# MLP of a two-layer decoder: the fourth block's down-projection feature by feature, the other three turned by VectorE and DMA

## The chip, the cores and the metric

The kernel runs on one core of a Trainium2 chip. The time is device microseconds (us) of that core, median of the runs shown. All numbers of the trace come from one profiled execution of the kernel.

## What is computed

A decoder of two layers over 256 tokens of 2048 features, all in float32. Each layer is a mixer (attention of one kind in layer 0, of another in layer 1), an MLP with squared ReLU, and a gated addition of a per-layer embedding. The part that the change touches is this, for each layer i:

```python
hn = rmsnorm(h, mlp_norm_g[i])
h = h + jnp.square(jax.nn.relu(hn @ mlp_w1[i])) @ mlp_w2[i]
gate = jax.nn.sigmoid(rmsnorm(h, ple_norm_g[i]) @ ple_w_gate[i])
h = h + (p[i] @ ple_w_proj[i]) * gate
```

mlp_w1 is 2048 x 8192, mlp_w2 is 8192 x 2048, ple_w_gate is 2048 x 2048 and ple_w_proj 256 x 2048.

## The kernel before

**Layout.** The residual stream x lies feature by feature: 16 tiles of 128 features by 256 tokens, two of them side by side in each of eight tiles xp[0] to xp[7] (L179, L180). Activations that enter a matmul are split in a high part in the type float32r and a low part (the rest), side by side in one tile of 512 columns (`split_to` L469, `renorm` L331). A product is high x high + high x low + low x high, all added up in PSUM.

**Weights.** Every weight is read once, in chunks of 128 x 1024 floats (512 KB). `load` (L198) fetches a chunk into one of four raw buffers through SP's queue; `copy` (L210) casts it on ScalarE to the high part (six buffers), and `sub` (L218) takes the low part on VectorE (five buffers). `Program.run` (L111) writes out the order by hand: for each chunk it first issues loads (at most seven chunks ahead, and only into a raw buffer whose subtraction has been issued), casts (four ahead) and subtractions (three ahead), then `advance` (L81) lets every follow-up generator that is under way take one step, then it issues the chunk's matmuls, and the follow-ups of a finished tile begin at the next chunk's step. A `yield` in a follow-up is thus a delay of one chunk. Nothing is reordered afterwards: each engine takes its instructions in that order, and SP takes its DMAs in that order too, each waiting for what it needs before the next one is looked at.

**Two forms of a projection.** `quad` (L376) goes feature by feature: the weights are the stationary operand, and four tiles of 128 features fill four PSUM banks over its chunks. A chunk gives 8 pairs of matmuls, one of 512 columns (L352: high weights by both parts of the activation) and one of 256 (L354: low weights by the high part). A bank ends with its two halves still to be added. `token_major` (L421) goes token by token: the activation is stationary and the weights move; two banks hold two halves of 128 tokens by 512 features, and a chunk gives 12 matmuls of 512 columns (L442). PSUM has two sets of four banks ("mm" and "at"), and each quad or token-major quarter takes the set that the one before didn't (`four_banks` L365, `two_banks` L415).

**The MLP** (`mlp`, L493) goes through the 8192 hidden features in four blocks of 2048. In each block four quads of eight chunks (w1) make 16 tiles h, and then four token-major quarters of eight chunks (w2) take these into 512 output features each. The sum over the blocks lies token by token in a tile y of 2 x 2048 floats a partition: ScalarE writes it for the first block (L504), VectorE adds the later ones (L502). In the fourth block `down` goes on for each quarter: eight transposes on TensorE against the identity (L513) into two banks of the other set, two adds to x of 512 columns on VectorE (L517), and then for each tile of x the renewed split and square for the next norm (`renorm`: L316 and L242 on ScalarE, L322 and L250 on VectorE). The transposes of a quarter are issued behind the second chunk of the next one, and those of the last quarter behind the second chunk of the next stage.

**The stage behind it** (`ple`, L559) goes through four quarters of: a quad of one chunk (the embedding's projection, pj tiles in pool "h", L723) and a quad of eight chunks (the gate). The gate's quad reads the renewed splits of x, and its norm's factor is worked out from chunk 4 on.

**The output projections of the mixers** (`out_proj`, L482) are quads whose follow-up is `add_to_x` (L474: two adds of 256 columns from PSUM into x) and `renorm`, with the third and fourth tile one step later (`late=True`). The profile has them in 449.81 to 483.09 us (layer 0, four chunks a quad).

Of the kernel before, what the change touches and what calls it, by code (L numbers as in the profile page):

```python
# [10 lines left out]
F32 = mybir.dt.float32  # L11
# [4 lines left out]
P = 128  # L16
D = 2048
T = 256
# [10 lines left out]
NFB = 4  # L29
# [9 lines left out]
G_ATTN, G_MLP, G_PLE, G_KV, G_FIN = 0, 2, 4, 6, 7  # L39
# [105 lines left out]
def kernel(ctx: ExitStack, tc: tile.TileContext, a: dict, out: bass.AP):  # L145
    nc = tc.nc
    ctx.enter_context(tc.manual_schedule())
    prog = Program()
# [4 lines left out]
    tmp = ctx.enter_context(tc.tile_pool(name="tmp", bufs=2))  # L153
    xap = ctx.enter_context(tc.tile_pool(name="xa", bufs=KT))
    wpool = ctx.enter_context(tc.tile_pool(name="w", bufs=4))
    pspool = ctx.enter_context(tc.tile_pool(name="ps", bufs=1, space=bass.MemoryType.PSUM))

    cur = {}

    def open_pool(key):  # L160
        es = ExitStack()
        cur[key] = es.enter_context(tc.tile_pool(name=key, reuse_waits="tile", bufs=1))
        cur[key + "/es"] = es

    def close_pool(key):
        cur.pop(key)
        cur.pop(key + "/es").close()

    def bank():
        return pspool.tile([P, 512], F32, tag="mm", name="mm", bufs=4)  # L170

    def banks2():
        return pspool.tile([P, 2, 512], F32, tag="at", name="at", bufs=2)
# [5 lines left out]
    xp = [xg0[:, :2 * T]] + [xpool.tile([P, 2 * T], F32, name=f"x{j}") for j in range(1, KT // 2)]  # L179
# [151 lines left out]
    def renorm(k, gi, to, norm):  # L331

        t = split_hi(k, gi)
        s = norm.square(k)
        yield
        split_lo(t, k, gi)
        to[k] = t
        norm.add(s)
# [76 lines left out]
    def two_banks(mm):  # L415
        if mm:
            return [bank(), bank()]
        b = banks2()
        return [b[:, 0, :], b[:, 1, :]]
# [54 lines left out]
    def add_to_x(k, ps):  # L474
        nc.vector.tensor_add(x[k], ps[:, :T], x[k])
        nc.vector.tensor_add(x[k], ps[:, T:], x[k])
# [15 lines left out]

    def mlp(layer, xg, norm, to, norm2):  # L493

        def down(b, q, ps0, ps1, mm):
            c = slice(q * 512, (q + 1) * 512)
            if b == q == 0:
                cur["y"] = cur["h"].tile([P, 2, D], F32, name=f"y{layer}")
            y = cur["y"]
            for j, ps in enumerate((ps0, ps1)):  # L500
                if b:
                    nc.vector.tensor_add(y[:, j, c], ps, y[:, j, c])  # L502
                else:
                    nc.scalar.copy(y[:, j, c], ps)  # L504
            if b < NFB - 1:
                return
            yield
            yield "tensor"
            tr = two_banks(not mm)
            for f in range(4):  # L510
                for j in range(2):
                    k = 4 * q + f
                    nc.tensor.transpose(tr[f // 2][:, (f % 2 * 2 + j) * P:(f % 2 * 2 + j + 1) * P],  # L513
                                        y[:, j, k * P:(k + 1) * P], ident)
            yield
            for i in range(2):
                nc.vector.tensor_add(xp[2 * q + i], tr[i], xp[2 * q + i])  # L517
            for i in range(2):
                yield
                both = [renorm(4 * q + 2 * i + f, G_PLE + layer, to, norm2) for f in range(2)]  # L520
                for g in both:
                    next(g)
                yield
                for g in both:
                    next(g, None)

        for b in range(NFB):
            h = [None] * 16
            for q in range(4):
                def done(f, ps, q=q, h=h):  # L530
                    t = sum_halves(ps)
                    yield
                    while norm.r is None:
                        yield
                    nc.vector.scalar_tensor_tensor(t, t, 0.0, norm.rb, op0=ALU.max, op1=ALU.mult)
                    yield
                    nc.scalar.activation(t, t, AF.Square)
                    ht = cur["h"].tile([P, 2 * T], F32R, tag="h", name="h", bufs=20)
                    yield from split_to(ht, t)
                    h[4 * q + f] = ht  # L540
                base = layer * 128 + (b * 4 + q) * 8
                quad(lambda c, base=base: a["w1"][base + c], KT, xg, done,
                     {4: [norm.factor]} if b == 0 and q == 0 else None, late=True,
                     twos=() if q else (0,) if b else (5,) if layer else ())
            for q in range(4):
                base = layer * 128 + (b * 4 + q) * 8
                token_major(lambda c, base=base: a["w2"][base + c], h,
                            lambda ps0, ps1, mm, b=b, q=q: down(b, q, ps0, ps1, mm), whole=True)

    def load_p(layer, to):  # L550
        for k in range(2):
# [7 lines left out]
    def ple(layer, pg, xg, norm, nxt, norm2, last):  # L559
        pj = [None] * KT  # L560
# [158 lines left out]
        for q in range(4):  # L719
            def proj_done(f, ps, q=q):  # L720
                s = tmp.tile([P, T], F32, tag="es", name="es", bufs=4)
                nc.scalar.copy(s, ps[:, :T])
                t = cur["h"].tile([P, T], F32, tag="pj", name="pj", bufs=8)  # L723
                nc.vector.tensor_add(t, ps[:, T:], s)
                pj[4 * q + f] = t
                return
                yield
            if q == 3 and last:
                pt = {}

                def pt_done(j, ps):
                    pt[j] = f32(cur["h"].tile([P, 2 * T], F32R, tag="h", name="h", bufs=20))
                    nc.scalar.copy(pt[j], ps)
                    return
                    yield
                parity[0] ^= 1
                token_major(lambda c: a["w_proj"][layer * 4 + q], pg, pt_done,
                            ring=bank if parity[0] else banks2, kt=2)
                last_quad(pt)
                return  # L740
            if q == 2 and last:
                prog.op(load_gain)
            quad(lambda c, q=q: a["w_proj"][layer * 4 + q], 2, pg, proj_done, twos=() if q else (0,))
            hooks = {4: [norm.factor]} if q == 0 else {}
            if q == 3 and not last:
                for c in range(6):
                    hooks[c] = [lambda k=k: split_x(k, G_KV, nxt) for k in (2 * c, 2 * c + 1)]
            quad(lambda c, q=q: a["w_gate"][layer * 32 + q * 8 + c], KT, xg,
                 lambda f, ps, q=q: gate_done(4 * q + f, ps), hooks)
# [185 lines left out]
    def start1():  # L935
        while x_kv[KT - 1] is None or n_b1.r is None:
            yield
        close_pool("h")
        open_pool("O")
        kvt["o0"] = cur["O"].tile([P, 2 * T], F32R, tag="ob", name="ob", bufs=HB // 2)  # L940
        for g in range(GB):
            kvt["k", g] = k_tile()
        open_pool("B")
        pb = cur["B"]
        value_tiles("vs", pb)
        kvt["vc"] = pb.tile([P, GB * DH], F32R, name="vc")
        nc.gpsimd.memset(f32(kvt["vc"]), 0.0)
        kvt["m0"] = pb.tile([P, P], F32, name="m0")
        kvt["m1"] = pb.tile([P, T], F32, name="m1")
        kvt["mc"] = pb.tile([P, 2, 2, 16], F32, name="mc")  # L950
        nc.gpsimd.dma_start(kvt["m0"], a["mB0"])
        nc.gpsimd.dma_start(kvt["m1"], a["mB1"])
        nc.gpsimd.dma_start(kvt["mc"], a["mC"])
        kvt["gs"] = pb.tile([P, 2, 64], F32, name="gs")
        for j in range(2):
            kvt["pc", j] = pb.tile([P, P], F32R, name=f"pc{j}")
            kvt["pcT", j] = pb.tile([P, T], F32R, name=f"pcT{j}")
            for n in ("pc", "pcT"):
                nc.gpsimd.memset(f32(kvt[n, j]), 0.0)
        for n in ("w2_k", "w2_v"):  # L960
            zt[n] = pb.tile([P, 2, DH], F32, name=n)
            nc.gpsimd.dma_start(zt[n], a[n])
        for n in ("rcC", "rcS"):
            zt[n] = pb.tile([64, 32], F32, name=n)
            nc.gpsimd.dma_start(zt[n], a[n])
        open_pool("C")
        pc = cur["C"]
        for n in ("rk", "rv"):
            zt[n] = pc.tile([P, GB * T], F32, name=n)
        for j in range(2):  # L970
            zt["z", j] = pc.tile([P, 8, 2, GB, 16], F32R, name=f"z{j}")
            nc.gpsimd.memset(f32(zt["z", j]), 0.0)
        for n in ("pe_k", "pe_v"):
            zt[n] = pc.tile([P, 32], F32, name=n)
            nc.gpsimd.dma_start(zt[n], a[n])
# [388 lines left out]
    ple(1, p1, x_p1, n_p1, None, n_fin, True)  # L1364

    prog.run(load, copy, sub)
    close_pool("h")


# [108 lines left out]
```

## Time and profile before

| | us |
|---|---|
| median of 3 runs | 2501.91 (2501.83 to 2502.07) |
| the profiled execution's own time | 2502.39 |
| its span, first to last instruction | 2500.6 |
| fourth block's down-projection, layer 0 | 1100.16 to 1189.92 |
| fourth block's down-projection, layer 1 | 2296.82 to 2386.57 |

Some lines of the page beside those that the prediction shows: the share of the DMA engines and what they moved, in 40 slices of the span (each 62.5 us).

```profile
DMA  8565555555656556656565744455555665665553
GB/s 274 176 199 190 175 169 181 180 190 190 192 193 193 189 191 194 192 189 187 187 196 188 245 160 124 146 191 188 193 193 191 191 192 192 193 191 190 185 187 130
```

In the page, PE is TensorE's matmuls, PEld its weight loads, DVE VectorE, ACT ScalarE, POOL GpSimd, and SP the engine that issues the DMAs. A row of the groups reads: line, engine, operation, out<-in, shapes, count, then busy us, mean ns of one, and the idle time of its engine ahead of it with what ended it. A row of the waits reads: who waited, for whom: us in total, times, the longest. A row of a single line's view gives the shortest, median and longest ns. A row of DMAs gives count, KB and the median us from issue to landing. In the timeline of PE a matmul's length overlaps with the next one's, so paces are taken from start to start.

### The profile page before, as it was taken

Reading aid. Unit: us, or ns where it says so; the run is one execution under the profiler, and the core shown is the slowest. Engines: PE = TensorE matmul, PEld = TensorE weight load, DVE = VectorE, ACT = ScalarE, POOL = GpSimd, SP = SyncE. Lnnn points to the kernel's source line nnn. Section 1 sums busy time; section 2 is a strip of 40 time slices with the busy share of each in tenths; the row PEclk is TensorE's granted clock in tenths of the full one; section 3 lists DMA queues with packets and bytes.
Section 4 is the critical chain, followed back from the end, with each engine's and each line's share of the span. In section 5 each row is a group of like instructions: output and inputs, shape, how many; then the busy total and the mean of one; then the engine's idle time right before and its main releaser. Section 6 shows DMA issues by size and latency. Waiting matters only on the chain.

```text
span 2500.6 us, 35900 instructions
## 1 busy us (share of the span) xinstructions
PE 2489.7 (100%) x13405; PEld 2144.8 (86%) x13405; DVE 1655.1 (66%) x2804; ACT 1346.8 (54%) x2162; POOL 10.4 (0%) x24
## 2 busy tenths in 40 slices
PE   9999999999999999999999999999999999999998
PEld 8888888888888888888888889988888888888887
DVE  7766676865465565566787989876546556556676
ACT  6444444554454453555664788755545445445455
POOL 0000000000000000000000000000000000000000
PEclk9999999999999999999999999999999999999999
DMA  8565555555656556656565744455555665665553
GB/s 274 176 199 190 175 169 181 180 190 190 192 193 193 189 191 194 192 189 187 187 196 188 245 160 124 146 191 188 193 193 191 191 192 192 193 191 190 185 187 130
DMA packets 131071, 468.47 MB, mean 187 GB/s; under 512 B 14736, under 2 KB 15696, under 8 KB 130896
## 3 DMA queue, kind: packets, MB, share of 16 engines
q1 hardware_dynamic: 129792, 464.31, 57.7%
q8 instruction: 105, 1.72, 0.3%
q0 software_dynamic: 528, 1.07, 0.1%
q10 hardware_dynamic: 576, 0.79, 0.1%
q14 instruction: 70, 0.57, 0.1%
HBM read 464.02 MB, written 2.10 MB: 186 GB/s over the span
## 4 chain that ended last, share of the span: by engine, by line
PE 97%; DMA 1%; DVE 1%; ACT 1%; issue 0%; SPq 0%; ACTq 0%; DVEq 0%
PE mm L352 22%; PE mm L442 18%; PE at L352 17%; PE at L442 15%; PE mm L354 11%; PE at L354 8%; DMA raw<-in_w_kv 1%; PE at L827 1%; PE at L1313 0%; DVE wlo L221 0%; PE mm L1337 0%; PE at L852 0%; PE mm L584 0%; PE mm L586 0%; PE mm L585 0%
## 5 line engine op out<-in xcount | busy, mean ns | idle before, releaser
L221 DVE TENSOR_TENSOR wlo<-raw,whi 128x1024 fp32r<-128x1024 f32 (+1 forms) x875 | 1065.6, 1219 | 632.4 <-PE at L442 131.8
L213 ACT CAST whi<-raw 128x1024 fp32r<-128x1024 f32 (+1 forms) x875 | 919.5, 1052 | 879.2 <-PE mm L442 200.0
L352 PE MATMUL mm<-xa,whi 128*128 128x512 f32 x2208 | 756.2, 395 | 0.0
L354 PE MATMUL mm<-xa,wlo 128*128 128x256 f32 x2208 | 575.2, 278 | 0.0
L352 PE MATMUL at<-xa,whi 128*128 128x512 f32 x1632 | 568.3, 394 | 0.0
L352 PEld LDWEIGHTS mm<-xa,whi 128*128 128x128 f32 x2208 | 399.2, 188 | 75.8 <-issue 0.4
L354 PE MATMUL at<-xa,wlo 128*128 128x256 f32 x1632 | 452.7, 277 | 0.0
L354 PEld LDWEIGHTS mm<-xa,wlo 128*128 128x128 f32 x2208 | 414.8, 188 | 20.4
L352 PEld LDWEIGHTS at<-xa,whi 128*128 128x128 f32 x1632 | 306.0, 187 | 70.4
L442 PE MATMUL at<-whi,h 128*128 128x512 f32 x1024 | 315.6, 389 | 0.0
L442 PE MATMUL mm<-whi,h 128*128 128x512 f32 x1024 | 315.5, 389 | 0.0
L354 PEld LDWEIGHTS at<-xa,wlo 128*128 128x128 f32 x1632 | 306.6, 188 | 0.1
L442 PEld LDWEIGHTS at<-whi,h 128*128 128x128 f32 x1024 | 191.9, 188 | 39.7
L442 PEld LDWEIGHTS mm<-whi,h 128*128 128x128 f32 x1024 | 191.5, 188 | 39.5
L442 PE MATMUL mm<-wlo,h 128*128 128x512 f32 x512 | 199.2, 389 | 0.0
L442 PE MATMUL at<-wlo,h 128*128 128x512 f32 x512 | 199.2, 389 | 0.0
L442 PEld LDWEIGHTS mm<-wlo,h 128*128 128x128 f32 x512 | 96.1, 188 | 20.0
L442 PEld LDWEIGHTS at<-wlo,h 128*128 128x128 f32 x512 | 96.1, 188 | 19.9
L360 DVE TENSOR_TENSOR et<-mm,es 128x256 f32<-128x256 f32 x137 | 55.9, 422 | 75.8 <-ACT es L358 73.9
L442 PE MATMUL mm<-whi,xa 128*128 128x512 f32 x320 | 98.9, 390 | 0.0
L358 ACT COPY es<-mm 128x256 f32<-128x256 f32 x137 | 48.4, 372 | 62.8 <-PE mm L354 59.9
L442 PEld LDWEIGHTS mm<-whi,xa 128*128 128x128 f32 x320 | 59.6, 188 | 12.3
(326 smaller groups left out, 2138.3 us busy)
## 6 DMA issues: line engine op xcount, KB each, us to landing
raw<-in_w SPq DMA_DIRECT2D x512, 512.0 KB, 3.5
raw<-in_w_qk SPq DMA_DIRECT2D x96, 512.0 KB, 3.6
raw<-in_w_gate SPq DMA_DIRECT2D x64, 512.0 KB, 4.0
raw<-in_w_kv SPq DMA_DIRECT2D x48, 512.0 KB, 4.2
raw<-in_w_v SPq DMA_DIRECT2D x47, 512.0 KB, 3.6
raw<-in_w_q SPq DMA_DIRECT2D x32, 512.0 KB, 4.5
raw<-in_w_oB SPq DMA_DIRECT2D x32, 512.0 KB, 3.5
raw<-in_w_oA SPq DMA_DIRECT2D x16, 512.0 KB, 3.5
```

The source lines that it names most:

```text
L213: nc.scalar.copy(hi[:, c], t[:, c])
L221: nc.vector.tensor_sub(lo[:, c], t[:, c], f32(hi)[:, c])
L352: nc.tensor.matmul(ps, hi[:, col:col + P], rhs, start=first, stop=False)
L354: nc.tensor.matmul(ps[:, :T], lo[:, col:col + P], rhs[:, :T], start=False, stop=last)
L358: nc.scalar.copy(s, ps[:, :T])
L360: nc.vector.tensor_add(t, ps[:, T:], s)
L442: nc.tensor.matmul(st[j], *parts[j][i], start=k == i == 0, stop=k == kt - 1 and i == 2)
L827: nc.tensor.matmul(sb[:, j, T + (g - 1) * P:T + g * P] if g else sb[:, j, :T], q[:, own], k[:, own] if g else k, start=True, stop=True)
```

## The change

Both layers' `mlp` change in the same way.

- **The fourth block's down-projection** is four quads of eight chunks in place of four token-major quarters. Their follow-up is that of the output projections: `add_to_x`, then `renorm`.
- **The sum of the first three blocks** stays token by token, in two tiles of half the features (two quarters each). When the third block has finished a half, VectorE turns its two token halves in blocks of 32 x 32 (one instruction of 128 x 1024 each, one step apart, into the new pool "z"). One step later SP writes both to a DRAM buffer (512 KB each); in the next step it issues the four reads of the first, in the step behind that the four reads of the second. A read fetches 32 partitions of 4 runs of 256 floats (128 KB). They land feature by feature in a tile of the shape of y (in the slot that y leaves). Two steps behind the second reads VectorE begins to add it to x: four adds of 128 x 512, one a step. The first half's turn falls into the third block's third and fourth quarters, the second half's into the fourth block's first up-projection quad and on.
- **The transposes on TensorE** (L513), the fourth block's adds to y (L502) and the adds from the turned banks to x (L517) are gone.
- **Pools**: "z" is open from the start to the end of an MLP; in its place the pj tiles get a pool "j" of their own.

```diff
+    dpool = ctx.enter_context(tc.tile_pool(name="bounce", bufs=1, space=bass.MemoryType.DRAM))
...
+    def bounce(src, name, to):
+        m = src.shape[1] // 4
+        d = dpool.tile([P, 4 * m], F32, tag=name, name=name, bufs=2)
+        nc.sync.dma_start(d, src)
+        yield
+        d4 = d.rearrange("(a s) (b n) -> b s a n", a=4, b=4)
+        for b in range(4):
+            nc.sync.dma_start(to[32 * b:32 * b + 32], d4[b])
...
     def mlp(layer, xg, norm, to, norm2):
+        prog.op(lambda: open_pool("z"))
+        y = {}
         def down(b, q, ps0, ps1, mm):
-            c = slice(q * 512, (q + 1) * 512)
-            if b == q == 0:
-                cur["y"] = cur["h"].tile([P, 2, D], F32, name=f"y{layer}")
-            y = cur["y"]
+            half, c = q // 2, slice(q % 2 * 512, (q % 2 + 1) * 512)
+            if b == 0 and q % 2 == 0:
+                y[half] = cur["h"].tile([P, 2, D // 2], F32, tag="y", name="y", bufs=2)
             for j, ps in enumerate((ps0, ps1)):
                 if b:
-                    nc.vector.tensor_add(y[:, j, c], ps, y[:, j, c])
+                    nc.vector.tensor_add(y[half][:, j, c], ps, y[half][:, j, c])
                 else:
-                    nc.scalar.copy(y[:, j, c], ps)
-            if b < NFB - 1:
+                    nc.scalar.copy(y[half][:, j, c], ps)
+            if b < NFB - 2 or q % 2 == 0:
                 return
-            yield
-            yield "tensor"
-            tr = two_banks(not mm)
-            for f in range(4):
-                for j in range(2):
-                    k = 4 * q + f
-                    nc.tensor.transpose(tr[f // 2][:, (f % 2 * 2 + j) * P:(f % 2 * 2 + j + 1) * P],
-                                        y[:, j, k * P:(k + 1) * P], ident)
-            yield
-            for i in range(2):
-                nc.vector.tensor_add(xp[2 * q + i], tr[i], xp[2 * q + i])
-            for i in range(2):
+            zs = []
+            for j in range(2):
                 yield
-                both = [renorm(4 * q + 2 * i + f, G_PLE + layer, to, norm2) for f in range(2)]
-                for g in both:
-                    next(g)
+                z = cur["z"].tile([P, D // 2], F32, tag="z", name="z", bufs=2)
+                nc.vector.transpose(z.rearrange("p (b t r) -> p t b r", b=4, r=32),
+                                    y[half][:, j].rearrange("p (t b s) -> p t b s", b=4, s=32))
+                zs.append(z)
+            w = cur["h"].tile([P, 8, T], F32, tag="y", name="yw", bufs=2)
+            yield
+            moves = [bounce(z, "dM", w[:, 4 * j:4 * j + 4]) for j, z in enumerate(zs)]
+            for g in moves:
+                next(g)
+            for g in moves:
                 yield
-                for g in both:
-                    next(g, None)
+                next(g, None)
+            yield
+            for n in range(4):
+                yield
+                xn = xp[4 * half + n].rearrange("p (f a r) -> p f a r", f=2, r=32)
+                wn = w.rearrange("p a (t r) -> p t a r", r=32)[:, 2 * n:2 * n + 2]
+                nc.vector.tensor_add(xn, wn, xn)
...
             for q in range(4):
                 base = layer * 128 + (b * 4 + q) * 8
-                token_major(lambda c, base=base: a["w2"][base + c], h,
-                            lambda ps0, ps1, mm, b=b, q=q: down(b, q, ps0, ps1, mm), whole=True)
+                if b < NFB - 1:
+                    token_major(lambda c, base=base: a["w2"][base + c], h,
+                                lambda ps0, ps1, mm, b=b, q=q: down(b, q, ps0, ps1, mm), whole=True)
+                    continue
+                def done(f, ps, q=q):
+                    add_to_x(4 * q + f, ps)
+                    yield
+                    yield from renorm(4 * q + f, G_PLE + layer, to, norm2)
+                quad(lambda c, base=base: a["w2"][base + c], 16, h, done, late=True)
+        prog.op(lambda: close_pool("z"))
+        prog.op(lambda: open_pool("j"))
```

In `ple` the pj tiles are taken from cur["j"] in place of cur["h"], and pool "j" is closed wherever "h" is.

## What was predicted

> **What bounds the kernel now.** I read the page first: the busy shares, the forty slices and the chain that ended last.
>
> ```profile
> span 2500.6 us, 35900 instructions
> PE 2489.7 (100%) x13405; PEld 2144.8 (86%) x13405; DVE 1655.1 (66%) x2804; ACT 1346.8 (54%) x2162; POOL 10.4 (0%) x24
> ...
> PEclk9999999999999999999999999999999999999999
> ...
> PE 97%; DMA 1%; DVE 1%; ACT 1%; issue 0%; SPq 0%; ACTq 0%; DVEq 0%
> ```
>
> TensorE holds 97% of the chain, and its granted clock is nine tenths or more in every slice. A busy PE proves little by itself, so the second look is at who waits for whom in the fourth down-projection of layer 0 (1100.16 to 1189.92 us), on the engines and on SP's queue.
>
> ```profile
> ACT whi L213 <- PE at L442: 20.1, 13, 1.7
> ACT whi L213 <- PE mm L442: 18.7, 13, 1.7
> DVE wlo L221 <- PE mm L442: 7.1, 5, 1.5
> DVE wlo L221 <- PE at L442: 6.0, 4, 1.5
> ...
> SPq L201 <- DVE wlo L221: 72.6, 30, 4.3
> ```
>
> ScalarE and VectorE wait for TensorE to give back buffers of split weights; SP waits for VectorE to give back raw ones. Everything stands queued behind TensorE. So the time of this stage is the number of matmuls times their pace, and the third look takes that pace from the timeline of PE, at the starts of the quarters (in columns: start, length, instruction).
>
> ```profile
> 449.81 0.40 PE L352 MATMUL at<-oT,whi 128*128 128x512 f32 x1
> ...
> 483.09 0.40 PE L352 MATMUL mm<-xa,whi 128*128 128x512 f32 x1
> ...
> 1077.98 0.40 PE L352 MATMUL at<-xa,whi 128*128 128x512 f32 x1
> ...
> 1100.16 0.40 PE L442 MATMUL mm<-whi,h 128*128 128x512 f32 x1
> ...
> 1121.93 0.62 PE L442 MATMUL at<-whi,h 128*128 128x512 f32 x2
> ...
> 1127.38 1.03 PE L513 MATMUL at<-ident,y 128*128 128x128 f32 x8
> 1128.17 0.70 PE L442 MATMUL at<-whi,h 128*128 128x512 f32 x2
> ...
> 1144.60 0.39 PE L442 MATMUL mm<-whi,h 128*128 128x512 f32 x1
> ...
> 1189.92 0.39 PE L352 MATMUL mm<-pg,whi 128*128 128x512 f32 x1
> ...
> 1195.13 0.39 PE L352 MATMUL at<-xa,whi 128*128 128x512 f32 x1
> 1195.36 0.28 PE L354 MATMUL at<-xa,wlo 128*128 128x256 f32 x1
> 1195.48 1.04 PE L513 MATMUL mm<-ident,y 128*128 128x128 f32 x8
> 1196.27 0.47 PE L352 MATMUL at<-xa,whi 128*128 128x512 f32 x1
> 1196.59 0.27 PE L354 MATMUL at<-xa,wlo 128*128 128x256 f32 x1
> ...
> 2296.82 0.40 PE L442 MATMUL mm<-whi,h 128*128 128x512 f32 x1
> ...
> 2386.57 0.39 PE L352 MATMUL mm<-pg,whi 128*128 128x512 f32 x1
> ```
>
> A quarter token by token with no transposes in it (1100.16 to 1121.93) takes 21.77 us: 8 chunks of weights, 96 matmuls of 512 columns, 2.72 us a chunk. A quarter feature by feature of the up-projection (1077.98 to 1100.16) takes 22.18: 8 chunks, 128 matmuls, 2.77 us a chunk. Both stream 6,144 columns a chunk; only the count of instructions differs, 12 against 16. The extra 0.05 us over four instructions makes a fixed cost of some 13 ns each.
>
> **The change, part by part.**
>
> *1. The fourth block feature by feature.* Its three later quarters each carry the eight transposes of the quarter before: 1121.93 to 1144.60 is 22.67, which is 0.90 over 21.77. The transposes are 0.79 of it (1127.38 to 1128.17) and the rest is the slower first matmul behind them. The whole block takes 1189.92 - 1100.16 = 89.76 us in layer 0 and 2386.57 - 2296.82 = 89.75 in layer 1. In its place come four quads of eight chunks. The nearest row for a quad that adds to x and renews the norm, as these will, is the output projection of the first mixer: 12 chunks of the same shape from 449.81 to 483.09, 2.773 us each, so 22.19 for eight and 88.75 for four. Each layer gains 1.0 here.
>
> *2. The last quarter's transposes*, which stand in the next stage: 1195.48 to 1196.27 is 0.79, and the matmul behind them takes 0.32 (1196.27 to 1196.59) instead of the 0.23 of the pair before (1195.13 to 1195.36): 0.88 a layer.
>
> Sum on TensorE: 1.01 + 0.88 and 1.00 + 0.88, together **-3.77 us**. In other words, eight groups of transposes give back about 7.1 us, and eight quads in place of token quarters take 8 x 0.42 = 3.4 of it away.
>
> *Why the pace of the quads should hold.* VectorE gets more to do in these quads, for the add to x is now two instructions of 256 columns for each of 16 tiles.
>
> ```profile
> 449.81:483.09 33.28, 33.28 (x194) 29.08 (x193) 31.93 (x59) 21.70 (x37) 0.00 (x0) 1.00 0.59 193
> ...
> L221 DVE TENSOR_TENSOR wlo<-raw,whi 128x1024 fp32r<-128x1024 f32 x12 | 14.7, 1224 | 0.8 <-ACT sq L242 0.4
> L322 DVE SCALAR_TENSOR_TENSOR xa<-x,gains,xa 128x256 fp32r<-128x256 f32 x12 | 5.7, 478 | 0.0
> L250 DVE TENSOR_TENSOR acc<-acc,sq 128x256 f32<-128x256 f32 x11 | 4.6, 418 | 0.0
> L475 DVE TENSOR_TENSOR x<-mm,x x16: 414/416/420, 448.4 to 1659.7; 128x256 f32<-128x256 f32 x16
> ...
> L502 DVE TENSOR_TENSOR y<-mm,y x24: 691/692/692, 769.9 to 2364.1; 128x512 f32<-128x512 f32 x24
> L517 DVE TENSOR_TENSOR x<-at,x x8: 680/686/694, 1128.5 to 2371.0; 128x512 f32<-128x512 f32 x8
> ```
>
> The first row is the output projection by window (span, then PE, PEld, DVE, ACT): VectorE is busy 31.93 of 33.28 us there, 96%, and TensorE still keeps 2.773. The new quads have eight chunks in place of four for the same tail: 32 subtractions x 1.22, 32 adds x 0.42, 16 x 0.48 and 16 x 0.42 make 67 us of 88.75, 75%. Out go eight adds to y and eight to x at 0.69, 11 us. So VectorE is no bound; I cost this at nothing. If that cover were gone, each us by which VectorE falls behind after its lead (below) would be a us on TensorE.
>
> *3. The turn by VectorE and DMA, during the fourth block.* For each half of the features: two block transposes of 128x1024 on VectorE, two writes of 512 KB to DRAM, eight reads of 128 KB back in runs of 1 KB, four adds of 128x512. All are new, and none is on TensorE; what they can cost is delay on VectorE, SP and DMA, so the question is how much delay is covered. A weight chunk's low part has five buffers: the subtraction for chunk n starts when TensorE has done with n-5, four chunks ahead of its use, and ends 4 x 2.72 - 1.22 = **9.7 us ahead**. The load of chunk n is issued when the subtraction of n-4 is over, 8 x 2.72 - 1.22 = 20.5 us ahead. Take off the landing, the cast and the subtraction:
>
> ```profile
> raw<-in_w SPq DMA_DIRECT2D x512, 512.0 KB, 3.5
> ...
> out<-h SPq DMA_DIRECT2D x5, 256.0 KB, 2.0
> ...
> ps<-in_pT POOLq DMA_DIRECT2D x4, 128.0 KB, 2.9
> ...
> q1 hardware_dynamic: 129792, 464.31, 57.7%
> ...
> L213 ACT CAST whi<-raw 128x1024 fp32r<-128x1024 f32 x33 | 34.8, 1055 | 40.4 <-PE at L442 20.1 <-PE mm L442 18.7 <-ACT sq L242 1.6
> L201 SPq DMA_DIRECT2D raw<-in_w x512: 327/328/349, 462.6 to 2362.7; - x171
> ```
>
> 20.5 - 3.5 - 1.05 - 1.22 = **14.7 us** by which SP or DMA may hold the loads before TensorE feels it.
>
> - *Block transposes*: no row shows one. From below, the subtraction of the same 1024 columns, 1.22; from above twice that, since the pattern is broken into runs of 32. They stand in two different steps, behind that step's subtraction; 1.22 + 2.44 is 3.66 against a step of 2.72, so at worst VectorE falls 1.9 us behind of its 9.7. Cost on TensorE 0.
> - *Writes*: between the 2.0 us of 256 KB out and the 3.5 of 512 KB in; I take 3.5 to 4.5 with two writes and a load together.
> - *Reads*: 2.9 us is the row for 128 KB; eight can overlap. SP's order at a half is load, two writes, load, four reads, load, four reads. The first reads wait for the first write, so SP stands some 4 us; the next load is due 5.5 us after the writes and is held back about a us by ten issues of 0.33. Queued behind SP are weight loads alone, with 14.7 us of cover.
> - *DMA share*: 464.31 MB in 57.7% of 2500.6 us is 322 MB a ms at full use. A half moves 2 MB besides four loads of 0.5 MB in the four steps (11 us) between its writes and its first add: 4.2 MB by bytes is 13 us, so the queues run full and end some 2 us late. If runs of 1 KB cost as much as the 4 KB runs of the loads, the reads take four times as long and everything is some 9 us later. Late by 2 to 11, against 14.7 for the loads.
> - *Adds*: the first stands seven steps behind the half's end on VectorE, 13.6 us after the writes; what waits behind it there is the subtractions, with 9.7 us of lead. Reads landed later than 13.6 + 9.7 = 23.3 us after the writes would cost TensorE time.
>
> So part 3 costs 0 by my reading; from above, the bound is the second rival's price. Nothing makes it a gain, since TensorE waits for none of it now.
>
> *4. Pools.* The turned y takes the slot of the y it came from, and the pool z closes long after its last write; no wait at the end. 0.
>
> **Sum**: -3.77 us against the profiled execution's own 2502.39 us (span 2500.6 and 1.8 around it), which is 0.48 above the median; carried to the median, 2501.91 - 3.8 = **2498.1 us**, -0.15%.
>
> **The rivals.**
>
> *A. A seam.* After the last new quad comes a projection of one chunk, and then a quad in the banks that the last quad filled. The third and fourth tiles' adds stand one step later: after TensorE's end VectorE has a subtraction, and the four adds of 0.42, done about 3 us later if it is on time, and needed at 2.77 + 6 x 0.35 = 4.8. Only if VectorE is over 1.8 us behind does TensorE wait, by perhaps 1 us a layer; with a first matmul slowed at the new seams I set the whole at 0.5 to 3: 2498.6 to 2501, still within 0.2%.
>
> *B. The reads come one after another* (the side that is slower). Writes at 3.5 each and eight reads at 2.9 make 2 x 3.5 + 8 x 2.9 = 30.2 us, which passes 23.3 by 6.9; four halves cost 27.6, so 2501.9 - 3.8 + 27.6 = **2525.7**. It decides from 23.3 us on. For it: nothing in this trace reads 1 KB runs into 32 partitions. Against it: 16 DMA engines serve one queue, and loads of 512 KB land in 3.5. The Trainium skill, "DMA: Bandwidth & Descriptors" (Rules for kernel authors; Anatomy of one DMA), speaks for it: two transfers to disjoint partitions serialize, and some 2 us of each DMA is the receipt, heaviest towards HBM. No run here shows such a pair yet.
>
> *C. The transposes cost nothing now*, because TensorE fills a wait with them. Then only the +3.4 of the quads is left: 2505.3. Against it: the quarters without them are 0.90 shorter, and no wait of PE stands there.
>
> *D. The extra instructions of the quads cost nothing here*, because weight loads and matmuls overlap better than in the up-projection. Then nothing is taken off the 7.1 us of the transposes: 2501.9 - 7.1 = 2494.8. Against it: the quads of two stages in the rows above agree on 2.77 a chunk. The Trainium skill, "TensorE: Matmul & The Clock Gate" (Wait — 56ns, not 53.3ns?), gives each matmul some 2.5 ns beyond its columns; by it four more a chunk would cost 10 ns and the time would be about 2495.4. The trace disagrees, with 13 ns for each.
>
> **How the numbers follow.** Forecast 0.70, A 0.14, B 0.07, C 0.04, D 0.03; 0.02 for what I have not seen, halved between the sides. About 0.2% (5 us) is what a measurement of this kernel can tell from no change. Forecast, A and C are within it: 0.88. Faster: D and 0.01, 0.04. Slower: B and 0.01, 0.08. The range 2496.8 to 2501.5 holds the forecast, with 1.3 us below it, and A: 0.84.
>
> **What would show it.** In the timeline of PE: the fourth block's quads at 22.19 each, 88.75 a layer, no L513, and the quad after the one-chunk projection without a gap. In the waits: ScalarE and VectorE still waiting for PE, and at most four waits of VectorE's add to x for the reads, under 9 us each. Wrong, if PE has gaps about 20 us behind a write, if the reads land over 23 us after the writes, if the last quad's adds come over 1.8 us late, or if the new quads run at 22.4 or more.

## The result, and the profile after

The changed kernel takes 2498.27 us (median of 22 runs, 2497.95 to 2499.04), the kernel before 2501.99 (median of 22 runs taken beside them, 2501.51 to 2502.18): 3.72 us less, a ratio of 0.9986 with an interval of 0.998 to 0.9992, which leaves out 1. The profiled execution took 2498.41 us (before: 2502.39). Its page:

```profile
span 2496.6 us, 36379 instructions
PE 2486.0 (100%) x13597; PEld 2151.9 (86%) x13597; DVE 1675.3 (67%) x2860; ACT 1345.8 (54%) x2162; POOL 10.3 (0%) x24
...
PE 98%; DVE 1%; ACT 0%; issue 0%; DMA 0%; ACTq 0%; DVEq 0%
```

TensorE has 192 matmuls more (256 more from the quads, 64 transposes fewer), less time, and still the whole chain. The timeline of PE, at the starts of the fourth block's first two quads, of the stage behind it and of that stage's first two gate quads, and then the block's start and end in layer 1:

```profile
1100.14 0.40 PE L366 MATMUL mm<-h,whi 128*128 128x512 f32 x1
1122.33 0.40 PE L366 MATMUL at<-h,whi 128*128 128x512 f32 x1
...
1188.89 0.40 PE L366 MATMUL mm<-pg,whi 128*128 128x512 f32 x1
1191.68 0.40 PE L366 MATMUL at<-xa,whi 128*128 128x512 f32 x1
...
1217.53 0.39 PE L366 MATMUL at<-xa,whi 128*128 128x512 f32 x1
...
2294.78 0.40 PE L366 MATMUL mm<-h,whi 128*128 128x512 f32 x1
2383.52 0.40 PE L366 MATMUL mm<-pg,whi 128*128 128x512 f32 x1
```

A quad takes 22.19 us and the block 88.75 and 88.74, in place of 89.76 and 89.75. The gate's quad starts 2.79 us behind the block's end, with no transposes in it and no wait. Each layer gives 1.01 us in the block. The rest comes from behind it: from the block's end to the start of the second gate quad it was 29.61 us before (1189.92 to 1219.53) and is now 28.64 (1188.89 to 1217.53), 0.97 less. The second gate quad before:

```profile
1219.53 0.39 PE L352 MATMUL at<-xa,whi 128*128 128x512 f32 x1
```

The first write of the first half's turn in layer 0 is issued at 973.16 us. First the window from there to the first add (span, PE, PEld, DVE, ACT, POOL, granted clock, DMA share, GB/s); then SP's DMAs, VectorE's first add with its wait in brackets, and the median landings:

```profile
973.16:991.04 17.88, 17.88 (x81) 14.80 (x80) 6.76 (x6) 5.27 (x5) 0.00 (x0) 1.00 0.97 256
```

```profile
973.16 3.20 SPq L180 DMA_DIRECT2D dM<-z  x2
976.76 0.33 SPq L215 DMA_DIRECT2D raw<-in_w  x1
979.68 1.76 SPq L184 DMA_DIRECT2D yw<-dM  x4
981.54 0.39 SPq L215 DMA_DIRECT2D raw<-in_w  x1
981.97 1.97 SPq L184 DMA_DIRECT2D yw<-dM  x4
```

```profile
991.04 0.69 DVE L546 TENSOR_TENSOR x<-yw,x 128x512 f32<-128x512 f32 x1 [5.37 <-DMA raw<-in_w]
```

```profile
dM<-z SPq DMA_DIRECT2D x8, 512.0 KB, 6.3
yw<-dM SPq DMA_DIRECT2D x32, 128.0 KB, 4.2
```

The DMA engines are 97% busy for 18 us, VectorE stands idle for 5.4 us ahead of its first add, and TensorE is busy throughout: the turn is not cheap, but it is covered. The profile puts VectorE's wait down to a weight load, but the add reads what all eight reads bring, and the last of them, issued at 983.51 us, landed 7.2 us later, at 990.7, just ahead of the add.

### The profile page after: what moved, and what is told of

The parts are those of the page before. It is cut to its first block, busy times and chain, and to the rows that moved or that the text cites. A ratio compares the mean times of both kernels' runs of the same rounds, so it can differ in the third digit from the quotient of the medians.

```text
span 2496.6 us, 36379 instructions
## 1 busy us (share of the span) xinstructions
PE 2486.0 (100%) x13597; PEld 2151.9 (86%) x13597; DVE 1675.3 (67%) x2860; ACT 1345.8 (54%) x2162; POOL 10.3 (0%) x24
## 3 DMA queue, kind: packets, MB, share of 16 engines
q0 software_dynamic: 528, 1.07, 0.2%
## 4 chain that ended last, share of the span: by engine, by line
PE 98%; DVE 1%; ACT 0%; issue 0%; DMA 0%; ACTq 0%; DVEq 0%
PE mm L366 25%; PE at L366 19%; PE mm L456 15%; PE mm L368 12%; PE at L456 12%; PE at L368 10%; PE at L858 1%; PE at L1345 0%; PE mm L1369 0%; DVE wlo L235 0%; PE at L883 0%; PE mm L615 0%; PE mm L617 0%; PE mm L616 0%; PE at L1295 0%
## 5 line engine op out<-in xcount | busy, mean ns | idle before, releaser
L456 PE MATMUL mm<-whi,h 128*128 128x512 f32 x768 | 236.6, 389 | 0.0
L456 PE MATMUL at<-whi,h 128*128 128x512 f32 x768 | 236.5, 389 | 0.0
L456 PEld LDWEIGHTS at<-whi,h 128*128 128x128 f32 x768 | 144.2, 188 | 29.9
L456 PEld LDWEIGHTS mm<-whi,h 128*128 128x128 f32 x768 | 143.8, 188 | 29.7
L456 PE MATMUL mm<-wlo,h 128*128 128x512 f32 x384 | 149.5, 389 | 0.0
L456 PE MATMUL at<-wlo,h 128*128 128x512 f32 x384 | 149.5, 389 | 0.0
L366 PE MATMUL at<-h,whi 128*128 128x512 f32 x256 | 88.9, 394 | 0.0
L366 PE MATMUL mm<-h,whi 128*128 128x512 f32 x256 | 88.9, 394 | 0.0
L456 PEld LDWEIGHTS mm<-wlo,h 128*128 128x128 f32 x384 | 72.1, 188 | 15.0
L456 PEld LDWEIGHTS at<-wlo,h 128*128 128x128 f32 x384 | 72.1, 188 | 14.9
```

The source lines that it names most:

```text
L366: nc.tensor.matmul(ps, hi[:, col:col + P], rhs, start=first, stop=False)
L456: nc.tensor.matmul(st[j], *parts[j][i], start=k == i == 0, stop=k == kt - 1 and i == 2)
```

## The experiments

**1. Without the turn.** The sum of the first three blocks is left out of x.

```diff
-            if b < NFB - 2 or q % 2 == 0:
-                return
+            return
```

> The changed kernel without the turn: the sum of the first three blocks is made token by token but never turned nor added to x, so no block transposes, no writes to DRAM, no reads, no adds. Theory (the turn is fully hidden): the same time as the changed kernel, 2498.3 us, within 0.5. Rival (part of the turn is paid on TensorE): each half costs something, and this kernel is faster by four times that; at 1 us a half it would be 2494.3.

Measured 2498.16 us (2497.61 to 2501.34), against 2498.27 with the turn. All of the turn's instructions and 8 MB of traffic together cost nothing that can be told from zero.

**2. The turn on TensorE.** Everything else as in the changed kernel.

```diff
-            if b < NFB - 2 or q % 2 == 0:
+            if b < NFB - 2:
                 return
...
+            tr = two_banks(mm if q == 3 else not mm)
+            for f in range(4):
+                for j in range(2):
+                    k = 4 * (q % 2) + f
+                    nc.tensor.transpose(tr[f // 2][:, (f % 2 * 2 + j) * P:(f % 2 * 2 + j + 1) * P],
+                                        y[half][:, j, k * P:(k + 1) * P], ident)
```

> The fourth block feature by feature as in the changed kernel, but the sum of the first three blocks is turned by TensorE as before (eight groups of eight transposes and two adds of 512 columns each, during the third block and the start of the fourth). Theory (each group costs TensorE 0.88 to 0.90 us): 2498.3 + 7.1 = 2505.4 us, slower than before by 3.4. Rival C of the prediction (the transposes cost nothing): 2498.3. In the trace, quarters of the third block at 22.67 us by the theory, at 21.77 by the rival.

Measured 2505.32 us (ratio to before 1.0013, interval 1.0004 to 1.0022): 7.05 us over the changed kernel, for eight groups of transposes. In its timeline of PE, the third block's second quarter from start to end:

```profile
945.71 0.39 PE L456 MATMUL at<-whi,h 128*128 128x512 f32 x1
...
968.38 0.39 PE L456 MATMUL mm<-whi,h 128*128 128x512 f32 x1
```

22.67 us, as the theory has it. Rival C is out, and it is taking the transposes off TensorE that brings the gain: with the quads, and the transposes still on TensorE, the kernel is slower than before.

**3. All blocks feature by feature.** No y and no turn; each quad adds to x.

```diff
+                def done(f, ps, b=b, q=q):
+                    add_to_x(4 * q + f, ps)
+                    if b < NFB - 1:
+                        return
```

> All four blocks' down-projections feature by feature, each quad adding to x at once; no y, no turn. 24 more quads in place of token-major quarters than in the changed kernel. Theory (0.42 us a quad, 13 ns for each extra matmul): 2498.3 + 24 x 0.42 = 2508.4 us. Rival D of the prediction (extra instructions nearly free, 10 ns a chunk): 2498.3 + 24 x 0.08 = 2500.2. If VectorE's two adds a tile were a bound, over 2508.4.

Measured 2518.55 us (2518.45 to 2519.47; ratio 1.0067, interval 1.0054 to 1.0079): 20.3 over the changed kernel, where 10.1 was the theory's. The timeline of PE has no gaps in the quads, but layer 0 has two paces, here at the starts of the last quad of the first block and of the three behind it:

```profile
639.37 0.39 PE L366 MATMUL at<-h,whi 128*128 128x512 f32 x1
...
661.55 0.39 PE L366 MATMUL mm<-xa,whi 128*128 128x512 f32 x1
...
684.14 0.40 PE L366 MATMUL at<-xa,whi 128*128 128x512 f32 x1
...
706.75 0.40 PE L366 MATMUL mm<-xa,whi 128*128 128x512 f32 x1
```

22.18, then 22.59 and 22.61, and so on to the end of the MLP of layer 0: 24 quads at 0.42 more, which are the other 10 us. At 661.55 stands the second block's first quad, whose first chunk has another order: for two tiles the two matmuls with high weights and then the two with low ones (`twos` in `quad`), in place of high, low, high, low. The first quads of the third and fourth block begin so too.

In layer 1 the same order stands in the same three places, and the quads keep the faster pace. Here is its second block's first quad and the start of the next one, 22.19 us apart:

```profile
1872.05 0.39 PE L366 MATMUL mm<-xa,whi 128*128 128x512 f32 x1
...
1894.24 0.40 PE L366 MATMUL at<-xa,whi 128*128 128x512 f32 x1
```

What differs there is that the first quad of the whole MLP already has the order, in its sixth chunk (the `(5,)` in the next edit).

**4. The same without that order** in the later blocks.

```diff
-                     twos=() if q else (0,) if b else (5,) if layer else ())
+                     twos=() if q or b else (5,) if layer else ())
```

> All four blocks' down-projections feature by feature, as in the kernel before with all quads (2518.55 us), but the first up-projection quad of the later blocks no longer begins with the order hi, hi, lo, lo in its first chunk. In that kernel every quad took 22.19 us up to that chunk of the second block and 22.6 behind it. Theory (quads have two paces, and the order of one chunk, put behind quads instead of token-major quarters, brings the slower): all quads at 22.19 us, 2508.4 us. Rival (the slower pace comes from the load on VectorE by two adds a tile in every block): still some 2518.5.

Measured 2509.08 us (2508.63 to 2509.6; ratio 1.0028, interval 1.0017 to 1.0039). Only in layer 0 was there a slower pace to take away.

```profile
661.48 0.39 PE L366 MATMUL mm<-xa,whi 128*128 128x512 f32 x1
...
683.66 0.39 PE L366 MATMUL at<-xa,whi 128*128 128x512 f32 x1
...
705.85 0.39 PE L366 MATMUL mm<-xa,whi 128*128 128x512 f32 x1
```

All quads of the down-projections take 22.18 to 22.19, and so do those of the up-projections in the later blocks. So in layer 0 the order of three chunks (the first quad of each later block) decides the pace of the 543 us from 661 to 1204, and VectorE's load, which is the same in both kernels, does not. With this, 24 quads more cost 10.8 us, 0.45 each (0.42 was predicted), and rival D is out: the extra matmuls cost what the rows said.

**5. and 6. More token-major quarters: a half, and three quarters of the features.** Their turn ends in the fourth block or behind it, and the turned tiles of x are renewed there. The edit for the half:

```diff
-            if b < NFB - 2 or q % 2 == 0:
+            if b < NFB - 1 - half or q % 2 == 0:
...
                 nc.vector.tensor_add(xn, wn, xn)
+                if half == 0:
+                    prog.waiting.append(renew(n))
...
-                if b < NFB - 1:
+                if b < NFB - 1 or q < 2:
```

> The first half of the features goes token by token through all four blocks and is turned during the fourth block's third and fourth quarters (then added to x and renewed); only the second half's fourth block is feature by feature. Two quads a layer go back to token-major quarters. Theory (0.42 us a quad, turn hidden): 2498.3 - 4 x 0.42 = 2496.6 us. Rival (the turn's delays now reach the next stage, which needs the renewed x): no gain or a loss, over 2498.3.

> The first three quarters of the features go token by token through all four blocks: the first two are turned together as in the kernel with a half, the third quarter alone (half the size) during the fourth block's last quarter; only the last quarter's fourth block is a quad. Theory (0.42 us a quad, turn hidden): 2498.3 - 6 x 0.42 = 2495.8 us. Rival (the third quarter's renewed x comes too late for the gate's fifth chunk): a gap of TensorE in each layer and no gain over the kernel with a half.

Measured 2500.98 us for the half (2499.9 to 2501.59; ratio 0.9996, interval 0.9987 to 1.0004) and 2513.42 for three quarters (2510.78 to 2515.44; ratio 1.0046, interval 1.0033 to 1.0058): both missed the theory. In the kernel with a half, the first quad behind the token-major quarters and the next one (1143.57 to 1166.17 is 22.60), and a wait in the gate's quad:

```profile
1143.57 0.39 PE L366 MATMUL mm<-h,whi 128*128 128x512 f32 x1
...
1166.17 0.40 PE L366 MATMUL at<-h,whi 128*128 128x512 f32 x1
...
1192.87 0.28 PE L368 MATMUL at<-xa,wlo 128*128 128x256 f32 x1
1193.99 0.47 PE L366 MATMUL at<-xa,whi 128*128 128x512 f32 x1 [0.84 <-DVE x L490]
```

The quads have the slower pace, and the wait is rival A's seam: the bank waits for VectorE's add to x (L490). The kernel misses its theory by 4.4 us: the slower quads are 4 x 0.42 = 1.7 of it, and from the block's end to the second gate quad the timeline has 1.5 us more than the changed kernel in layer 0 and 1.4 in layer 1. With three quarters, the stage behind waits for a renewed tile (ScalarE's square, L256) in the place where the seam is:

```profile
1190.51 0.40 PE L368 MATMUL mm<-pg,wlo 128*128 128x256 f32 x2
1194.55 0.76 PE L366 MATMUL at<-xa,whi 128*128 128x512 f32 x1 [3.65 <-ACT sq L256]
```

**7. The half, with the order high, high, low, low** at the start of the fourth block's quads.

```diff
-                quad(lambda c, base=base: a["w2"][base + c], 16, h, done, late=True)
+                quad(lambda c, base=base: a["w2"][base + c], 16, h, done, late=True, twos=(0,) if q == 2 else ())
```

> The kernel with half of the features token by token in all four blocks (2500.98 us), with the order hi, hi, lo, lo in the first chunk of the quad that follows token-major quarters in the fourth block. There the two quads took 22.6 us each. Theory of two paces: this order is what a quad behind token-major quarters needs, so the quads take 22.19, 4 x 0.42 = 1.7 us less, about 2499.3 us, with the two gaps of about 1 us ahead of the gate's quad still there since VectorE is late. Rival (the pace comes from VectorE's load): no change, 2501.

Measured 2500.34 us (2498.97 to 2501.55).

```profile
1143.57 0.39 PE L366 MATMUL mm<-h,whi 128*128 128x512 f32 x1
...
1165.75 0.40 PE L366 MATMUL at<-h,whi 128*128 128x512 f32 x1
...
1192.51 0.28 PE L368 MATMUL at<-xa,wlo 128*128 128x256 f32 x1
1193.85 0.47 PE L366 MATMUL at<-xa,whi 128*128 128x512 f32 x1 [1.07 <-DVE x L490]
```

The quad is back at 22.18, but the time hardly moved: the medians differ by 0.6 us where 1.7 was expected, and the two ranges overlap, so that even the 0.6 is not clear of noise. In layer 0 the wait grew to 1.07 and another of 0.25 stands ahead of the gate's quad; in layer 1 they are 1.07 and 0.46, where the kernel of experiment 5 has one of 0.69. VectorE is not done earlier than it was, and TensorE comes earlier.

**8. The same order in the changed kernel's fourth block**, where a quad precedes.

```diff
-                quad(lambda c, base=base: a["w2"][base + c], 16, h, done, late=True)
+                quad(lambda c, base=base: a["w2"][base + c], 16, h, done, late=True, twos=() if q else (0,))
```

> The changed kernel, with the order hi, hi, lo, lo in the first chunk of the first quad of the fourth block's down-projection. Nothing else differs: the same matmuls, on the same data. Theory of two paces (this order behind a quad brings the slower one): eight quads at 22.6 in place of 22.19, 2498.3 + 8 x 0.42 = 2501.7 us, which takes the change's gain away, and more if the slower pace lasts into the gate's quad. Rival (pace not set by the order): 2498.3.

Measured 2498.24 us (2497.99 to 2499.39), no change, and the quads stay at 22.19. The theory in this form falls: the order does not slow every quad that follows a quad. It did so where the quads before had run without it (3, layer 0), and it did no harm where they had it already (here, and 3, layer 1). One reading that fits these runs is that the pairs of matmuls keep a rhythm that an earlier change of order set, and that only some changes leave it good; no run shows such a rhythm, and which changes those are, the runs don't settle.

**9. Longer turns, to find the end of the cover.** One copy of 512 KB from DRAM to DRAM between write and reads, for the second token half, for both, and two for both.

```diff
+        for i in range(hops):
+            e = dpool.tile([P, 4 * m], F32, tag=f"{name}{i}", name=f"{name}{i}", bufs=2)
+            nc.sync.dma_start(e, d)
+            d = e
```

> The changed kernel with one more copy from DRAM to DRAM (512 KB) between the write and the reads of the second token half of each turn, so that its reads are issued some 6 us later. The changed kernel's reads land 17.9 us after the writes, and the cover ends at 23 (adds at 12.5 after the writes, and 9.7 of lead). Theory (a cover with a sharp end): landing at 21 to 24 us, so 0 to 1 us a half, 2498.3 to 2501.5 us. Rival (no cover; every us of delay is paid): 6 us in each of four halves, 2522.

> One more copy from DRAM to DRAM (512 KB) between the write and the reads of both token halves of each turn; the second copy is issued behind the reads of the first. Theory (cover ends 22 to 23 us after the writes): reads land some 12 us later than 17.9, about 28 to 30 after the writes, so 5 to 8 us a half are paid, 2518 to 2530 us. Rival (no cover): 4 x 12 = 48 us, 2546. Rival (the delay never reaches TensorE): 2498.3.

> Two more copies from DRAM to DRAM between the write and the reads of both token halves. Theory: another 12 us of delay over the kernel with one copy each, now all beyond the cover, so it costs 4 x 12 = 48 us more than that kernel: some 2566 to 2578 us. The slope beyond the cover is 1 us of TensorE for each us of delay.

Measured 2498.09 us (2497.72 to 2498.76), 2505.85 (2503.7 to 2509.88; ratio 1.0016, interval 1.0007 to 1.0025) and 2536.8 (2534.59 to 2539.31; ratio 1.0136, interval 1.012 to 1.0151). VectorE's first add of the first turn, with its wait in brackets, one fence for each kernel in this order:

```profile
992.93 0.69 DVE L550 TENSOR_TENSOR x<-yw,x 128x512 f32<-128x512 f32 x1 [7.38 <-DMA yw<-dM]
```

```profile
995.99 0.69 DVE L550 TENSOR_TENSOR x<-yw,x 128x512 f32<-128x512 f32 x1 [10.70 <-DMA yw<-dM]
```

```profile
1004.74 0.69 DVE L550 TENSOR_TENSOR x<-yw,x 128x512 f32<-128x512 f32 x1 [18.96 <-DMA yw<-dM]
```

The first writes of the three were issued at 973.02, 972.77 and 973.26 us, so the add came 19.9, 23.2 and 31.5 us behind them. The prediction had set the end of the cover at 23.3. At 19.9 nothing is paid. At 31.5 the excess over 23.3 is 8.2; the timeline of PE in the kernel with two copies:

```profile
997.90 0.61 PE L460 MATMUL at<-whi,h 128*128 128x512 f32 x2
1006.63 0.80 PE L460 MATMUL at<-wlo,h 128*128 128x512 f32 x1 [8.11 <-DVE wlo L239]
```

TensorE stood for 8.11 us. The other three halves of this kernel have waits of 7.51, 6.40 and 6.17 us, 28.2 with the first, in a profiled execution that took 40.9 us more than that of the changed kernel; the clock behind the waits (last section) and a slower pace in layer 0 are part of the rest. My expectations of the size were too high, because I had each further copy for both halves add 12 us: the first moved the add by 5.3 (17.9 to 23.2), the second by 8.3. In the kernel with one copy the second half's copy is issued just behind the first half's reads, and can run beside them.

At 23.2, the edge, 7.6 us are paid, and hardly any of it is waiting. The timeline of PE in the kernel with one copy for both, at the starts of the fourth block's second to fourth up-projection quads and at the largest gap of that layer:

```profile
1033.56 0.40 PE L370 MATMUL at<-xa,whi 128*128 128x512 f32 x1
...
1041.88 0.40 PE L370 MATMUL at<-xa,whi 128*128 128x512 f32 x1
1042.58 0.39 PE L372 MATMUL at<-xa,wlo 128*128 128x256 f32 x1 [0.31 <-DVE wlo L239]
...
1056.49 0.40 PE L370 MATMUL mm<-xa,whi 128*128 128x512 f32 x1
...
1079.10 0.40 PE L370 MATMUL at<-xa,whi 128*128 128x512 f32 x1
```

The quad with the gap takes 22.93 us, and the next 22.61, and so do the rest of the MLP. Up to a wait of 0.31 us the chunks have the faster pace, and soon behind it the slower one; in layer 1 the same happens behind a wait of 0.62 in the same quad. Six quads a layer at 0.42 are 5.1 of the 7.6. That the wait is the cause is read from the order of time alone, and not every wait does it: in the kernel with two copies, 7.51 us of waiting in that quad of layer 0 are followed by the slower pace, and 6.17 us in that quad of layer 1 by 22.19 a quad.

**10. One quarter token by token in all four blocks.** Only the first quarter of the features goes token by token through all four blocks, and the quad behind it begins high, high, low, low. VectorE then has two quads to catch up.

```diff
+            part, q0, n4, blocks = ((0, 0, 4, 4), (1, 1, 4, 3), (2, 2, 8, 3), (2, 2, 8, 3))[q]
...
+                if b < NFB - 1 or q < 1:
...
+                quad(lambda c, base=base: a["w2"][base + c], 16, h, done, late=True, twos=(0,) if q == 1 else ())
```

> Only the first quarter of the features goes token by token through all four blocks; it is turned alone (half the size) during the fourth block's second quarter, and the other three quarters are as in the changed kernel (quads in the fourth block, the first with the order hi, hi, lo, lo in its first chunk). One quad a layer goes back to a token-major quarter, and VectorE has the last two quads to catch up. Theory (0.42 us a quad, no gap ahead of the gate's quad since VectorE is on time there): 2498.3 - 2 x 0.42 = 2497.4 us. Rival (VectorE still late at the next stage, as in the kernel with a half): 2498.3 or more.

Measured 2497.23 us (2497.08 to 2497.99; ratio to before 0.9982, interval 0.9973 to 0.9991), where the theory had 2497.4: 1.0 us less than the changed kernel. In PE's timeline the gate's quad starts without a wait, 2.79 us behind the block's end:

```profile
1188.47 0.40 PE L366 MATMUL mm<-pg,whi 128*128 128x512 f32 x1
...
1191.26 0.40 PE L366 MATMUL at<-xa,whi 128*128 128x512 f32 x1
```

## Why the prediction was right, step by step

**The sum.** -3.77 was forecast, -3.72 measured. The block (step 1) came out at 88.75 and 88.74 us for 88.75. Two terms of the sum were each tested alone: eight groups of transposes at 7.1, measured 7.05 (experiment 2), and 0.42 for each quad in place of a token quarter, measured 0.45 over 24 of them (experiment 4). The Trainium skill ("TensorE: Matmul & The Clock Gate", Wait — 56ns, not 53.3ns?) gives each matmul about 2.5 ns beyond its columns. That does not hold here: 0.42 us for 32 more matmuls a quad are 13 ns each.

Behind the block (step 2) the timeline gives 0.97 and 0.96 us a layer where 0.88 was forecast, and the two profiled executions differ by 3.98 us; that the medians come within 0.05 of the forecast is partly luck. The prediction also took a change under 5 us as one that can't be told from none; with 22 runs of each kernel 3.72 could be told.

**The turn's terms.** Of the unknown costs, the block transpose came out at the lower end (this is the row of L530, 1.22 to 2.44 was the range).

```profile
L530 DVE STREAM_TRANSPOSE z<-y x8: 1235/1238/1243, 970.4 to 2210.8; 128x1024 f32<-128x1024 f32 x8
```

The DMA terms were mis-sized: writes landed after 6.3 us (3.5 to 4.5 taken), reads after 4.2 (2.9), and the first add came 17.9 us behind the writes and not 13.6. Four waits of VectorE's add for the reads, under 9 us each, were among the signs given; there are four, the longest 5.4. The 13.6 was a little off too: VectorE was ready for the first add 12.5 us behind the writes (991.04 - 5.37 = 985.67). The end of the cover held: 31.5 less the 8.11 that TensorE stood is 23.4 (experiment 9). None of it reached TensorE, as experiment 1 shows; the cover had been worked out from the buffers and not from the landings, and 17.9 is inside it. The weight loads issued behind the writes, at 976.76 and 981.54 us, are of 512 KB too and landed after 6.4 us each, against a median of 3.8 for such loads in the whole trace; the two writes took 6.5 and 6.8. That points to the full DMA engines (97% busy in that window) and not to anything that only a write has. The Trainium skill ("DMA: Bandwidth & Descriptors", Anatomy of one DMA) says, of DMAs issued by GpSimd, that the receipt is most of a fixed 2 us and heaviest towards HBM. These DMAs are SP's, and no receipt can be told from their landings.

**Rival A** was no factor in the changed kernel: the last add to x in layer 0 ended 3.2 us behind TensorE's end at 1188.89, where about 3 was predicted:

```profile
1191.67 0.42 DVE L490 TENSOR_TENSOR x<-at,x 128x256 f32<-128x256 f32 x1
```

The mechanism is real, though: it shows as soon as VectorE is later (experiments 5 to 7). **Rival B** had its point of decision in the right place, 23.3 us (experiment 9), but the reads overlap: the eight of the first turn, at 2.9 one after another, would have taken 23 us, and all had landed 11 us after the first was issued (979.68 to 990.7). **C** and **D** are out by experiments 2 and 4.

**What the prediction took for granted.** It carried the pace of 22.19 from other quads, argued for it from VectorE's load, and named 22.4 as what would make it wrong, without knowing that quads have a second pace that VectorE's load does not set. At 22.6 the eight quads would have cost 3.4 us more and the change would have moved next to nothing. The fourth block's quads follow up-projection quads that already ran at 22.19, and kept it. That part of the prediction was right by luck: nothing in it argues for it.

## What to carry to other kernels

Where one engine holds the whole chain, count its instructions at the pace of the same shape in the same trace; that gave 3.77 for 3.72. For what is moved to other engines, work out the cover from the buffers (how many steps ahead does each stage run?), and compare landings with it: as long as the detour's end stays inside the cover, its length costs nothing. And check after a change that the pace behind it is still the one that was measured: here a changed order shifted it, and perhaps a short wait did.

## What the runs showed of the hardware

**A second pace of matmul pairs.** Pairs of 512 and 256 columns go at 22.19 or 22.61 us for 128 matmuls (173.3 or 176.6 ns each), with no gap and at a granted clock of 1.00 (experiment 3, 661 to 1204 us and layer 1). The order in a few chunks can set the slower one (2518.55 against 2509.08 us, experiments 3 and 4), and in experiment 9 it came behind waits of 0.31, 0.62 and 7.51 us, though not behind one of 6.17. In experiment 3 it lasted the 543 us to the end of layer 0's MLP; the gate's later quads take 22.19 again. Why, the runs don't show.

**The clock after a long wait.** In the kernel with two copies the window behind the 8.11 us of waiting, with the window ahead of the wait and one later (span, PE, PEld, DVE, ACT, POOL, granted clock, DMA share, GB/s):

```profile
990.00:998.00 8.00, 8.00 (x37) 6.64 (x36) 0.00 (x0) 1.05 (x1) 0.00 (x0) 1.00 0.79 249
...
1006.60:1010.00 3.40, 3.37 (x8) 2.67 (x9) 3.05 (x5) 2.09 (x2) 0.00 (x0) 0.53 0.87 346
1010.00:1020.00 10.00, 10.00 (x45) 8.26 (x44) 7.00 (x7) 5.23 (x5) 0.00 (x0) 1.00 0.79 262
```

The granted clock is 0.53 for the first 3.4 us, then 1.00, so this wait costs some 1.6 us more than itself (3.4 x 0.47). Others cost more: behind the 6.40 us of waiting in layer 1 it is 0.50 for 3.4 us and 0.69 for the next 4.4, and that quarter takes 31.31 us in place of 21.76, 3.15 more than the wait. With three quarters of the features (experiment 6) it is 0.50 for 2.95 us behind the wait of 3.65. In the windows around the waits of 0.31, 0.84 and 1.07 us in layer 0 of experiments 9, 5 and 7 the granted clock stays at 1.00.
